# The first loop of a diffusion-transformer layer: adaLN columns, rstd and order of products rearranged

## The chip, the cores and the metric

The kernel runs on one core of one Trainium2 chip. The metric is the device time of one execution in microseconds (us); lower is better. A profiled execution also has a span, from its first to its last recorded instruction, which is a little shorter than its time. The engines are PE (matrix products; PEld is its weight load), DVE (VectorE), ACT (ScalarE), POOL (GpSimd) and SP (here only a queue that issues transfers).

## What is computed

One layer over 512 latent tokens and 256 context tokens of width 1024, in float32: a half-step SwiGLU feed-forward, a token mixing step (latent attention beside a gated MLP), and a second feed-forward. Each sublayer first normalises its input and then scales and shifts it (adaLN). Scale, shift and gate come from a conditioning vector c for the latent tokens and from a constant c_ctx for the context. The change touches only the beginning:

```python
mx = split((silu(c) @ w_ada + b_ada)[:, None, :], 9)          # latent: shift, scale, gate, ...
mc = split((silu(c_ctx) @ w_ada + b_ada)[None, None, :], 9)   # context
h = x * rsqrt(mean(x * x) + eps) * norm1_w
h = h * (1 + scale) + shift
x = x + 0.5 * gate * ((silu(h @ w1) * (h @ w3)) @ w2)         # width 1024 -> 2816 -> 1024
```

## The kernel before

Everything is kept transposed: the width of 1024 is cut into 8 tiles of 128 partitions (the index k or d below), and tokens lie along the free dimension, 512 latent and 256 context ones. A float32 product is made from three fast ones: each operand is split into a high part (a cast, on ScalarE) and a low part (a subtraction, on VectorE), and high x high, high x low and low x high are summed in PSUM. The names end in h and l: oph and opl for weights, hh and hl for the normalised input. The products of small float32 matrices that are not split run as two instructions each.

**Start (L253 to L307, L473 to L505).** SP's queue loads x's latent columns, then for tiles 0, 1 and 2 a block of w_ada (scale half and shift half, 1024 numbers a partition each) and a piece of the first feed-forward weights (wfirst), then the context columns of x. Meanwhile PE spreads c and c_ctx over all partitions (L478: 32 instructions with 128x128 weights), and ScalarE copies the result into cb (put_cb). ScalarE and VectorE square x, and PE adds over the width by a product with a matrix of ones (L486). So the sum of squares of each token stands in all 128 partitions, and rstd_start and rstd_end make rsqrt on arrays of 128x512.

**One adaLN tile d.** The scale of 128 output columns, for both conditioning vectors, is a row product (ada_row, L317): the weights are silu(c) and silu(c_ctx), 2 columns, and the moving operand is the block of w_ada, 128 wide; for d in ROWS2 = (1, 2, 3) the block holds the shift too and is 256 wide. The 2-row result is copied by ScalarE (ada_copy), turned into columns by PE with an identity (ada_col, L329), and gets bias and factor on ScalarE. For the other d the shift is a dot product on VectorE, one for each conditioning vector (ada_dot, 128x1024 with an accumulator, called junk in the profile).

**The first loop (L529 to L574).** It walks over k and makes the first two of the 22 feed-forward tiles: four latent products of 512 tokens with three parts each (first_mm, L524), which need hh and hl of tile k. For tile k + 1 VectorE multiplies x by scale and rstd (hfull), ScalarE adds the shift and casts (hh), VectorE makes hl. The context does the same one or two tiles at a time from k = 3 on (ctx_h), and its products (first_ctx, L517, 24 an iteration) come behind the latent products of the iteration after. The context's squares are made at k = 1 and 2 and added on VectorE; their sum over the width is taken on PE at k = 3 (L537).

**What sets the order.** The whole loop is written with the order of VectorE, ScalarE and GpSimd pinned (nc.ordered), and PE's instructions pinned one by one (pin). Each engine runs its own list in order, and a wait holds all that stands behind it on that engine. Buffers set when transfers start: two 1 MB blocks and one more in a side pool for w_ada, three raw buffers for weights; and there are five pairs of split weights (OPS), so the cast of tile 5 needs the pair that tile 0's context products read. SP issues its transfers in order too; an issue whose buffer is still in use holds the ones behind it.

After the loop come the rest of the first feed-forward, the mixing and the second feed-forward, where PE works almost without a gap. Their first product, in the profile, is the L60 row of PE at 76.06 us.

Of the kernel before, what the change touches and what calls it, by code (L numbers as in the profile page):

```python
# [17 lines left out]
P = 128  # L18
D = 1024
NK = D // P  # L20
# [6 lines left out]
EPS = 1e-6  # L27
# [5 lines left out]
NFIRST = 2  # L33
ROWS2 = (1, 2, 3)
W1 = 2 * NFIRST * P
NPLAIN1 = 4
NPLAIN2 = 4
BLOCKS = 2
# [4 lines left out]
COL_B, COL_N1, COL_N2, COL_N3 = 0, 72, 80, 88  # L43
# [130 lines left out]
def layer_kernel(ctx: ExitStack, tc: tile.TileContext, xT, wfirst, wst, wada, wuq, wkpe, cols, wrope, vnw, rope, out):  # L174
# [25 lines left out]
    def mm():  # L200
        return ps.tile([P, 512], F32, tag="mm", bufs=4, name=f"mm_{nc.next_id()}")
# [54 lines left out]
    for k in range(0, NK, 2):  # L256
        load_x(k, 2, slice(0, 256))

    def first_units(k):
        r, rw = st.block(wada, k, sp if k % 3 == 2 else None), st.raw()  # L260
        nc.sync.dma_start(rw[:, :W1], wfirst[k])
        return r, rw

    u0, rw0 = st.raw_pool.tile([P, 2048], F32, tag="block", bufs=BLOCKS, name="block_first"), st.raw()
    nc.sync.dma_start(u0[:, :D], wada[0][:, :D])
    nc.sync.dma_start(u0[:, D:], wada[0][:, D:])
    nc.sync.dma_start(rw0[:, :W1], wfirst[0])
    units = [(u0, rw0), first_units(1)]
    units.append(first_units(2))
# [43 lines left out]
    def ada_row(r, d, kts=range(NK)):  # L313
        n = 2 * P if d in ROWS2 else P
        o = pa[0:2, :n]
        for kt in kts:
            pin(nc.tensor.matmul(o, sc[:, kt, :], r[:, kt * n : kt * n + n], start=kt == 0, stop=kt == NK - 1))  # L317
        return o

    def ada_copy(o, d):  # L320
        n = o.shape[1]
        row = sp.tile([2, 2 * P], F32, tag="row", name=f"row_{d}")[:, :n]
        nc.scalar.copy(row, o)
        return row

    def ada_col(row, d):
        o = [pcol[:, 4 * d + 2 * i : 4 * d + 2 * i + 2] for i in range(2)]
        for i in range(2 if d in ROWS2 else 1):
            pin(nc.tensor.matmul(o[i], row[:, i * P : i * P + P], ident[0:2, 0:2], start=True, stop=True))  # L329
        nc.scalar.activation(  # L330
            pairs[0][1][:, d, :], o[0], AF.Identity, bias=b1n[:, d : d + 1], scale=col[:, COL_N1 + d : COL_N1 + d + 1])
        if d in ROWS2:
            nc.scalar.activation(pairs[0][0][:, d, :], o[1], AF.Identity, bias=col[:, d : d + 1])

    def ada_shift(r, d, alone=False):
        for which in range(2) if d not in ROWS2 else ():
            ada_dot(r[:, D:], d, which, accs[:, d, which : which + 1])
            if alone:
                nc.scalar.activation(mod_s[0][which][:, d : d + 1], accs[:, d, which : which + 1], AF.Identity, bias=col[:, d : d + 1])
            yield  # L340
        if not alone and d not in ROWS2:
            nc.scalar.activation(pairs[0][0][:, d, :], accs[:, d, :], AF.Identity, bias=col[:, d : d + 1])
# [95 lines left out]
    def square0(which, k, on_vector=False):  # L438
        sel, n, _ = parts[which]
        sq = sp.tile([P, n], F32, tag=f"sqx{which}", bufs=4 if which == 0 else NK, name=f"sq0_{which}{k}")  # L440
        if on_vector:
            nc.vector.tensor_mul(two(sq), sel(x, k), sel(x, k))
        else:
            nc.scalar.activation(two(sq), sel(x, k), AF.Square)
        return sq

    def rstd_start(which, pt):
        n = parts[which][1]
        t = lambda s: sp.tile([P, n], F32, bufs=1, name=f"{s}{which}")
        r0, v = t("r0"), t("v")  # L450
        nc.scalar.activation(r0, pt, AF.Abs_reciprocal_sqrt, bias=epsc, scale=1.0 / D)
        return pt, r0, v

    def rstd_end(pt, r0, v):
        nc.vector.scalar_tensor_tensor(v, pt, EPS * D, r0, ALU.add, ALU.mult)
# [4 lines left out]
    def first_x(k, which):  # L460
        sel = parts[which][0]
        nc.vector.scalar_tensor_tensor(sel(hf, k), sel(x, k), mod_a[0][which][:, k : k + 1], two(rs[which]), ALU.mult, ALU.mult)

    def first_h(k, which):
        sel = parts[which][0]
        nc.scalar.activation(sel(hh, k), sel(hf, k), AF.Identity, bias=mod_s[0][which][:, k : k + 1])

    def first_l(k, which):
        sel = parts[which][0]
# [4 lines left out]
    pa, pcol = mm(), mm()  # L474
    bb = [big() for _ in range(2)]
    for w in range(2):
        for kt in range(NK):
            pin(nc.tensor.matmul(bb[w][:, kt // 4, (kt % 4) * P : (kt % 4) * P + P], sc[:, kt, w : w + 1].to_broadcast([P, P]), ident,  # L478
                                 start=kt % 4 == 0, stop=True, skip_group_check=True))
    sumx = mm()  # L480
    put_cb = lambda w: nc.scalar.copy(cb[:, w, :], bb[w].rearrange("p g c -> p (g c)"))
    for k in range(0, NK, 2):
        sa = square0(0, k)
        sb = square0(0, k + 1, k in (2, 6))
        nc.vector.tensor_add(sa, sa, sb)
        pin(nc.tensor.matmul(sumx, ones, sa, start=k == 0, stop=k == NK - 2))  # L486
    put_cb(0)
    nc.vector.tensor_scalar_add(b1, col[:, COL_B : COL_B + 72], 1.0)
    nc.vector.tensor_mul(b1n, b1[:, NK : 2 * NK], col[:, COL_N1 : COL_N1 + NK])
    r0 = rstd_start(0, sumx)  # L490
    row = ada_copy(ada_row(units[0][0], 0), 0)
    shift = ada_shift(units[0][0], 0, True)
    next(shift)
    rs = [rstd_end(*r0)]
    ada_col(row, 0)
    ops = {}

    first_x(0, 0)
    ops[0] = st.operand(units[0][1][:, :W1])
    first_h(0, 0)  # L500
    first_l(0, 0)
    ada_row(units[1][0], 1, range(4))
    put_cb(1)
    for _ in shift:
        pass  # L505
# [14 lines left out]
    def first_mm(k, i):  # L520
        uh, ul = ops[k]
        c = slice(i * P, i * P + P)
        for m, (l, r) in enumerate(((uh, hh), (uh, hl), (ul, hh))):
            pin(nc.tensor.matmul(two(pbs[i]), l[:, c], lat(r, k), start=k == 0 and m == 0, stop=k == NK - 1 and m == 2))  # L524

    ctx_h = {3: (0, 1), 4: (2, 3), 5: (4, 5), 6: (6, 7)}
    sqx = {1: 4, 2: 8}
    sqs = []
    for k in range(NK):  # L529
        if k + 3 < NK:  # L530
            units.append(first_units(k + 3))
        later = k + 2 < NK
        for i in range(NFIRST):
            first_mm(k, i)
        if k == 3:
            sumx = mm()[:, :256]
            pin(nc.tensor.matmul(sumx, ones, sqs[0], start=True, stop=True))  # L537
        if k == 0:
            row = ada_copy(ada_row(units[1][0], 1, range(4, NK)), 1)
            first_mm(0, NFIRST)  # L540
        if k + 1 < NK:
            ada_col(row, k + 1)
        if later:
            o = ada_row(units[k + 2][0], k + 2)
        for i in range(NFIRST + (k == 0), 2 * NFIRST):
            first_mm(k, i)
        shift = ada_shift(units[k + 2][0], k + 2) if later else iter(())
        next(shift, None)
        if k + 1 < NK:
            first_x(k + 1, 0)  # L550
            ops[k + 1] = st.operand(units[k + 1][1][:, :W1])
            first_h(k + 1, 0)
            next(shift, None)
            first_l(k + 1, 0)
        if later:
            row = ada_copy(o, k + 2)
        next(shift, None)
        if k == 3:
            rs.append(rstd_end(*rstd_start(1, sumx)))
# [6 lines left out]
        for j in ctx_h.get(k - 1, ()):  # L566
            first_ctx(j)
        if k in sqx:
            while len(sqs) < sqx[k]:
                sqs.append(square0(1, len(sqs)))  # L570
                if len(sqs) > 1:
                    nc.vector.tensor_add(sqs[0], sqs[0], sqs[-1])
        if k == 5:
            nc.scalar.activation(epsc2, epsc, AF.Silu)  # L574
# [1273 lines left out]
```

## Time and profile before

| | us |
|---|---|
| median of 3 runs | 1159.21 |
| lowest and highest run | 1158.89, 1159.34 |
| profiled execution, its own time | 1157.46 |
| its span | 1155.7 |
| first product of the first loop | 17.55 |
| first product behind the loop | 76.06 |

How to read the rows: in the order of time, a row has the start, the duration, the engine, the line, the operation with the tile it writes and the tiles it reads, and in brackets the idle time of that engine before it and what ended it. Many operations are recorded by a helper, so their line is L60 and the tile names tell them apart. In the rows by stretches, the columns are the length, then busy time and number of instructions of PE, PEld, DVE, ACT and POOL, the clock that PE was granted, the busy share of the transfer engines, and GB/s. In rows of groups, the numbers behind the bar are the busy time, the mean duration of one in ns, then the idle time before them and what ended it. PE's products overlap, so their durations add up to more than the time they take; the distance between starts is the price.

### The profile page before, as it was taken

Reading aid. Unit: us, or ns where it says so; the run is one execution under the profiler, and the core shown is the slowest. Engines: PE = TensorE matmul, PEld = TensorE weight load, DVE = VectorE, ACT = ScalarE, POOL = GpSimd, SP = SyncE. Lnnn points to the kernel's source line nnn. Section 1 sums busy time; section 2 is a strip of 40 time slices with the busy share of each in tenths; the row PEclk is TensorE's granted clock in tenths of the full one; section 3 lists DMA queues with packets and bytes.
Section 4 is the critical chain, followed back from the end, with each engine's and each line's share of the span. In section 5 each row is a group of like instructions: output and inputs, shape, how many; then the busy total and the mean of one; then the engine's idle time right before and its main releaser. Section 6 shows DMA issues by size and latency. Waiting matters only on the chain. (4 is left out here: it accounts for less than half of the span.)

```text
span 1155.7 us, 18702 instructions
## 1 busy us (share of the span) xinstructions
PE 1137.7 (98%) x7070; PEld 1069.7 (93%) x7070; DVE 904.5 (78%) x1670; ACT 532.7 (46%) x1075; POOL 321.6 (28%) x277
## 2 busy tenths in 40 slices
PE   9999999999999999999999999999999999999998
PEld 5699999999999999999988788999999989898997
DVE  4778989888988878867746969869876959686884
ACT  4454431441344213444735549876553535353441
POOL 0001402320433013300017636670013425152330
PEclk9999999999999999999999999999999999999999
DMA  9440244344234665312242101002221322233312
GB/s 346 150 157 24 92 146 147 109 145 154 103 128 146 222 205 170 133 64 68 83 146 91 57 35 56 20 1 76 72 92 55 134 86 77 106 110 110 110 37 92
DMA packets 34650, 125.89 MB, mean 109 GB/s; under 512 B 3584, under 2 KB 10496, under 8 KB 29056
## 3 DMA queue, kind: packets, MB, share of 16 engines
q1 hardware_dynamic: 34416, 124.63, 31.4%
q8 instruction: 56, 0.92, 0.3%
q14 instruction: 34, 0.28, 0.1%
q10 hardware_dynamic: 144, 0.06, 0.0%
HBM read 122.58 MB, written 2.10 MB: 108 GB/s over the span
## 5 line engine op out<-in xcount | busy, mean ns | idle before, releaser
L60 POOL TENSOR_TENSOR block<-block 128x512 f32<-128x512 f32 x69 | 104.9, 1520 | 395.8 <-DVE opl L60 393.1
L60 DVE TENSOR_TENSOR opl<-block,oph 128x512 fp32r<-128x512 f32 x216 | 184.0, 858 | 32.1 <-ACT oph L60 30.0
L60 ACT CAST oph<-block 128x512 fp32r<-128x512 f32 x216 | 133.8, 621 | 144.4 <-PE mm L60 99.1
L60 PE MATMUL mm<-gh,oph 128*128 128x384 f32 (+1 forms) x440 | 155.2, 353 | 0.0
L60 PE MATMUL mm<-gl,oph 128*128 128x384 f32 (+1 forms) x440 | 154.9, 352 | 0.0
L60 PE MATMUL mm<-gh,opl 128*128 128x384 f32 (+1 forms) x440 | 154.9, 352 | 0.0
L60 DVE SCALAR_TENSOR_TENSOR x<-mm,g,x 128x256 f32<-128x256 f32 (+2 forms) x184 | 82.8, 489 | 48.5 <-PE mm L60 47.8
L60 ACT CAST oph<-raw 128x512 fp32r<-128x512 f32 x106 | 64.5, 619 | 93.4 <-PE mm L60 74.5
L60 POOL TENSOR_TENSOR block<-s,block 128x512 f32<-128x512 f32 x35 | 48.2, 1378 | 153.8 <-DVE opl L60 153.1
L60 PEld LDWEIGHTS mm<-gh,oph 128*128 128x128 f32 x440 | 82.6, 188 | 5.7
L60 PEld LDWEIGHTS mm<-gh,opl 128*128 128x128 f32 x440 | 82.6, 188 | 5.6
L60 PEld LDWEIGHTS mm<-gl,oph 128*128 128x128 f32 x440 | 82.6, 188 | 5.5
L60 DVE TENSOR_TENSOR opl<-raw,oph 128x512 fp32r<-128x512 f32 x106 | 71.0, 683 | 11.7 <-ACT oph L60 11.2
L60 PE MATMUL mm<-hl,oph 128*128 128x384 f32 x192 | 64.3, 335 | 0.9 <-DVE hl L60 0.9
L60 PE MATMUL mm<-hh,oph 128*128 128x384 f32 x192 | 64.5, 336 | 0.0
L60 PE MATMUL mm<-hh,opl 128*128 128x384 f32 x192 | 64.1, 334 | 0.0
L60 DVE SCALAR_TENSOR_TENSOR junk<-raw,cb 128x1024 bf16<-128x1024 f32 x48 | 63.2, 1331 | 0.0
L60 POOL TENSOR_TENSOR s<-block 128x512 f32<-128x512 f32 x34 | 51.1, 1504 | 19.8 <-DMA block<-wst 19.8
L60 PE MATMUL one<-hh,oph 128*128 128x384 f32 x144 | 48.1, 334 | 0.0
L60 PE MATMUL one<-hl,oph 128*128 128x384 f32 x144 | 48.1, 334 | 0.0
L60 PE MATMUL one<-hh,opl 128*128 128x384 f32 x144 | 48.1, 334 | 0.0
L60 DVE SCALAR_TENSOR_TENSOR raw<-raw,cb 128x1024 f32<-128x1024 f32 x32 | 41.0, 1287 | 7.6 <-DMA raw<-wada 7.4
(649 smaller groups left out, 3462.7 us busy)
## 6 DMA issues: line engine op xcount, KB each, us to landing
raw<-wst SPq DMA_DIRECT2D x77, 512.0 KB, 3.7
block<-wst SPq DMA_DIRECT2D x36, 1024.0 KB, 4.9
raw<-wada SPq DMA_DIRECT2D x56, 512.0 KB, 4.1
block<-wada SPq DMA_DIRECT2D x7, 1024.0 KB, 7.2
x<-xT SPq DMA_DIRECT2D x6, 512.0 KB, 7.0
raw<-wfirst SPq DMA_DIRECT2D x8, 256.0 KB, 6.2
out<-x SPq DMA_DIRECT2D x7, 256.0 KB, 2.5
block_first<-wada SPq DMA_DIRECT2D x2, 512.0 KB, 8.1
```

Source lines behind the costliest of these rows:

```text
L60: return lambda *a, **k: self.tc.keep_in_program_order(f(*a, **k))
```

## The change

It has five parts, all in the start and the first loop.

1. Scale columns: the roles of the operands are exchanged. The 128x128 block of w_ada is now the weights and silu(c), silu(c_ctx) the 2-wide moving operand (ada_pe, L320 of the new file, 8 products of two instructions each), so that the column comes out as it is needed; row, copy and transposes go.
2. Shift columns: VectorE dots for every tile but d = 1 (SHIFT_PE), where PE makes them in the same way as the scale. The dots for the context are placed by a table (ctx_shift). Scale halves, shift halves and wfirst pieces are loaded by separate transfers into buffers of their own: three for scales, two of two shifts each.
3. rstd on tokens in partitions: the squares are the weights and a column of ones the moving operand (L443), so the sum of a token stands in one partition; rstd is made on 128x4 (128x2 for the context), and PE spreads it over the rows (over_rows, L457) into PSUM, where VectorE reads it for the latent tokens. The last tile's squares are halved between VectorE and ScalarE, and the last pair of x's loads is cut in two.
4. The products of tile 0 are taken in halves of 256 tokens (first_half, L543), with the columns of tile 1 between the halves.
5. For k = 4 to 6 the context products stand ahead of the latent products of the same iteration, no longer behind them.

Nothing behind the loop is edited. The diff, cut to its core:

```diff
-ROWS2 = (1, 2, 3)
+SHIFT_PE = (1,)
...
     def first_units(k):
-        r, rw = st.block(wada, k, sp if k % 3 == 2 else None), st.raw()
+        ra = sp.tile([P, D], F32, tag="sa", bufs=3, name=f"scale_{k}")
+        nc.sync.dma_start(ra, wada[k][:, :D])
+        if k % 2 == 0:
+            sblk.append(st.raw_pool.tile([P, 2048], F32, tag="block", bufs=BLOCKS, name=f"shift_{k}"))
+        rs_ = sblk[-1][:, (k % 2) * D : (k % 2) * D + D]
+        nc.sync.dma_start(rs_, wada[k][:, D:])
+        rw = st.raw()
         nc.sync.dma_start(rw[:, :W1], wfirst[k])
...
-    def ada_row(r, d, kts=range(NK)):
-        n = 2 * P if d in ROWS2 else P
-        o = pa[0:2, :n]
-        for kt in kts:
-            pin(nc.tensor.matmul(o, sc[:, kt, :], r[:, kt * n : kt * n + n], start=kt == 0, stop=kt == NK - 1))
-        return o
+    def ada_pe(d, part, dst, **kw):
+        o = pcol[:, 4 * d + 2 * part : 4 * d + 2 * part + 2]
+        r = units[d][part]
+        for kt in range(NK):
+            pin(nc.tensor.matmul(o, r[:, kt * P : kt * P + P], sc[:, kt, :], start=kt == 0, stop=kt == NK - 1))
+        nc.scalar.activation(dst[:, d, :], o, AF.Identity, **kw)
...
+    def ada_shift(d, which):
+        if d in SHIFT_PE:
+            if which == 0:
+                ada_pe(d, 1, pairs[0][0], bias=col[:, d : d + 1])
+            return
+        ada_dot(units[d][1], d, which, accs[:, d, which : which + 1])
+        nc.scalar.activation(mod_s[0][which][:, d : d + 1], accs[:, d, which : which + 1], AF.Identity, bias=col[:, d : d + 1])
...
+    def sums(sq, c0, first, last):
+        for t in range(sq.shape[1] // P):
+            pin(nc.tensor.matmul(stats[:, c0 + t : c0 + t + 1], sq[:, t * P : t * P + P], ones[:, 0:1],
+                                 start=first and t == 0, stop=last, skip_group_check=True))
+    def over_rows(dst, r):
+        for t in range(r.shape[1]):
+            pin(nc.tensor.matmul(dst[:, t * P : t * P + P], r[:, t : t + 1].to_broadcast([P, P]), ident,
+                                 start=t == 0, stop=True, skip_group_check=True))
...
+    ctx_shift = {0: (0,), 1: (2,), 3: (3,), 4: (4,), 5: (5,), 6: (6, 7)}
     for k in range(NK):
+        n = k + 1
         if k + 3 < NK:
-            units.append(first_units(k + 3))
+            first_units(k + 3)
+        if k == 0:
+            first_half(0)
+        if n < NK:
+            ada_scale(n)
+            ada_shift(n, 0)
         if k == 3:
-            sumx = mm()[:, :256]
-            pin(nc.tensor.matmul(sumx, ones, sqs[0], start=True, stop=True))
+            sums(sqs[0], 4, True, True)
+            rc = rstd_tok(4, 2)
+        if k == 0:
+            first_half(1)
+        elif n < NK:
+            for j in ctx_h.get(k - 1, ()):
+                first_ctx(j)
+            first_mm(k)
+        else:
+            first_mm(k)
+            for j in ctx_h[k - 1]:
+                first_ctx(j)
+        if k == 3:
+            over_rows(stats[:, 256:512], rc)
+        if n < NK:
+            if k < 3:
+                oph(n)
+                opl(n)
+            first_x(n, 0)
+            first_h(n, 0)
+            if k >= 3:
+                oph(n)
+            for j in ctx_shift.get(k, ())[:1]:
+                ada_shift(j, 1)
+            first_l(n, 0)
+            if k >= 3:
+                opl(n)
+        for j in ctx_shift.get(k, ())[1:]:
+            ada_shift(j, 1)
+        if k in (1, 2):
+            while len(sqs) < (NK // 2 if k == 1 else NK):
+                sqs.append(square0(1, len(sqs)))
+        if k == 2:
+            for sq in sqs[1:]:
+                nc.vector.tensor_add(sqs[0], sqs[0], sq)
...
         for j in ctx_h.get(k, ()):
             first_x(j, 1)
             first_h(j, 1)
```

More of the change, by code (lines that the diff above doesn't have):

```diff
@@ L255, in layer_kernel @@
     load_x = lambda k, n, c: nc.sync.dma_start(four(x[:, k : k + n, :], c), four(xT[:, k : k + n, :], c))
-    for k in range(0, NK, 2):
-        load_x(k, 2, slice(0, 256))
+    for k, n in ((0, 2), (2, 2), (4, 2), (6, 1), (7, 1)):
+        load_x(k, n, slice(0, 256))
+    sblk, units = [], []
     def first_units(k):
-        r, rw = st.block(wada, k, sp if k % 3 == 2 else None), st.raw()
[L261 to L269, printed above, removed]
+        ra = sp.tile([P, D], F32, tag="sa", bufs=3, name=f"scale_{k}")
[5 more added lines that the diff above has]
+        rw = st.raw()
+        nc.sync.dma_start(rw[:, :W1], wfirst[k])
+        units.append((ra, rs_, rw[:, :W1]))
+    for k in range(3):
+        first_units(k)
     for k in range(0, NK, 4):
@@ L326, in ada_col @@
[L326 to L333, printed above, removed]
@@ L473, in layer_kernel, with c_rows, oph, opl @@
     nc.ordered = True
-    pa, pcol = mm(), mm()
+    stats, pcol, spread = mm(), mm(), mm()
     bb = [big() for _ in range(2)]
-    for w in range(2):
-        for kt in range(NK):
+    def c_rows(w, kts):
+        for kt in kts:
             pin(nc.tensor.matmul(bb[w][:, kt // 4, (kt % 4) * P : (kt % 4) * P + P], sc[:, kt, w : w + 1].to_broadcast([P, P]), ident,
                                  start=kt % 4 == 0, stop=True, skip_group_check=True))
-    sumx = mm()
     put_cb = lambda w: nc.scalar.copy(cb[:, w, :], bb[w].rearrange("p g c -> p (g c)"))
-    for k in range(0, NK, 2):
+    c_rows(0, range(NK))
+    c_rows(1, range(4))
+    for k in range(0, 6, 2):
         sa = square0(0, k)
-        sb = square0(0, k + 1, k in (2, 6))
+        sb = square0(0, k + 1)
         nc.vector.tensor_add(sa, sa, sb)
-        pin(nc.tensor.matmul(sumx, ones, sa, start=k == 0, stop=k == NK - 2))
-    put_cb(0)
+        if k == 2:
+            put_cb(0)
+            c_rows(1, range(4, NK))
+        sums(sa, 0, k == 0, False)
     nc.vector.tensor_scalar_add(b1, col[:, COL_B : COL_B + 72], 1.0)
     nc.vector.tensor_mul(b1n, b1[:, NK : 2 * NK], col[:, COL_N1 : COL_N1 + NK])
[L490 to L495, printed above, removed]
-    ops = {}
[L498 to L505, printed above, removed]
+    for k in (6, 7):
+        sums(square0(0, k), 0, False, k == 7)
+    r0 = rstd_tok(0, 4)
+    put_cb(1)
+    ops = {}
+    def oph(k):
+        ops[k] = st.pair()
+        nc.scalar.copy(ops[k][0], units[k][2])
+    def opl(k):
+        nc.vector.tensor_sub(ops[k][1], units[k][2], ops[k][0].bitcast(F32))
+    ada_scale(0)
+    over_rows(spread, r0)
+    rs = [spread]
+    oph(0)
+    ada_shift(0, 0)
+    for g in range(2):
+        first_x(0, 0, g)
+        first_h(0, 0, g)
+    first_l(0, 0, 0)
+    opl(0)
+    first_l(0, 0, 1)
     pbs = bigs(4)
```

109 lines of the change are left out of this document (42 added, 67 removed).

## The prediction

> **What bounds the kernel now.** I read the page first, then busy time by stretches around the first loop, then the groups and waits inside it, then its order of time.
>
> ```profile
> span 1155.7 us, 18702 instructions
> PE 1137.7 (98%) x7070; PEld 1069.7 (93%) x7070; DVE 904.5 (78%) x1670; ACT 532.7 (46%) x1075; POOL 321.6 (28%) x277
> ```
> ```profile
> 0.00:17.55 17.55, 15.65 (x73) 9.85 (x73) 9.21 (x19) 10.40 (x19) 0.69 (x6) 1.00 0.92 334
> 17.55:76.06 58.51, 56.21 (x319) 40.15 (x319) 40.45 (x73) 26.71 (x62) 0.00 (x0) 1.00 0.57 198
> 76.06:1155.70 1079.64, 1065.85 (x6682) 1019.71 (x6680) 854.87 (x1580) 495.61 (x996) 320.89 (x271) 1.00 0.29 100
> ```
> ```profile
> L317 PE MATMUL mm<-block,sc 128*2 128x256 f32 x48 | 11.0, 379 | 0.1
> L317 PE MATMUL mm<-block,sc 128*2 128x128 f32 x64 | 7.6, 272 | 0.0
> L329 PE MATMUL mm<-ident,row 2*128 2x2 f32 x22 | 3.7, 254 | 0.3 <-ACT row L60 0.3
> ```
>
> PE is busy everywhere, so only what shortens PE's sequence, or a wait in it, moves the end. The change lies in the first two stretches: start-up (to 17.55) and the first loop (to 76.06, where the next stage's first product begins). In the loop PE is busy 56.2 of 58.5 us, and the rows above are what the change can take: the adaLN columns. Order of time for the loop's last third:
>
> ```profile
> 53.21 0.62 ACT L60 CAST oph<-raw 128x512 fp32r<-128x512 f32 x1 [3.46 <-PE mm L517]
> ```
> ```profile
> 56.41 0.50 PE L524 MATMUL big<-hl,oph 128*128 128x512 f32 x1 [1.42 <-DVE hl L60]
> ...
> 58.08 1.91 PE L317 MATMUL mm<-block,sc 128*2 128x128 f32 x16
> 59.92 0.50 PE L524 MATMUL big<-hh,oph 128*128 128x512 f32 x1
> ...
> 61.41 0.28 PE L517 MATMUL mm<-hh,oph 128*128 128x256 f32 x1
> ...
> 64.29 0.40 PE L524 MATMUL big<-hh,oph 128*128 128x512 f32 x1
> ...
> 76.06 0.34 PE L60 MATMUL mm<-hh,oph 128*128 128x384 f32 x1
> ```
>
> From starts, not durations (PE is pipelined): 24 context products (L517) take 64.29 - 61.41 = 2.88 us, 0.12 each; a scale row of 16 instructions takes 59.92 - 58.08 = 1.84. The first row shows a wait the order makes: the cast for tile 5 needs a buffer that the context products free; PE then waits 1.42 us for what follows from it.
>
> ```profile
> 26.48 0.50 PE L524 MATMUL big<-hh,oph 128*128 128x512 f32 x1
> ...
> 26.82 0.39 PE L524 MATMUL big<-hl,oph 128*128 128x512 f32 x1
> 27.05 0.40 PE L524 MATMUL big<-hh,opl 128*128 128x512 f32 x1
> ```
> ```profile
> 22.41 0.52 PEld L329 LDWEIGHTS mm<-ident,row 2*128 2x128 f32 x4 [0.36 <-ACT row L60]
> 22.94 3.11 PEld L317 LDWEIGHTS mm<-block,sc 128*2 128x2 f32 x16
> 26.48 0.19 PEld L524 LDWEIGHTS big<-hh,oph 128*128 128x128 f32 x1 [0.44 <-issue]
> ```
>
> A latent product takes 0.23 us (26.82 to 27.05), so a tile's twelve take 2.75; the first after a float32 group takes 0.34, and with the gap ahead of it the change of kind costs 0.24. Back to float32 I take 0.1, between two float32 groups 0.06.
>
> **The change, part by part.**
>
> *Price of the new operation.* Columns now come from 128x128 float32 weights and a 2-wide moving operand: 16 loads per column and 16 tiny products. Before has no such group. The nearest row is the four L329 loads above, also 128 columns wide and followed by 2-wide products: (0.52 - 0.184)/3 = 0.112 us a load, 0.184 being one load's duration. The other end is the wide broadcast loads:
>
> ```profile
> 4.87 3.61 PEld L478 LDWEIGHTS big<-ident,sc 128*128 128x128 f32 x27
> ```
>
> (3.61 - 0.19)/26 = 0.1315, with 128-wide products between; that is also my price for the added broadcasts. I take 0.112, the row with 2-wide products, for columns and sums: 1.8 us a column. So a scale column costs what the 128-wide row did (1.84); what goes is the L329 transposes, the ScalarE row copies, and the doubled rows of d = 1, 2, 3 (3.6 us from 22.94 to 26.48), of which only d = 1 keeps its shift on PE (a second 1.8).
>
> *Start-up.* The 32 broadcast pairs end at 8.5 on PE (the L478 row). Sums over d now have x's squares as weights: five groups of 8 loads, 40 x 0.112 + 5 x 0.06 = 4.8, gives 13.3. PE is never without them: the last square starts at 9.89, on x's landing, and now halved between ScalarE and VectorE is there by about 11.
>
> ```profile
> 9.89 0.63 ACT L60 ACTIVATE sq<-x 128x512 f32<-128x512 f32 x1 [0.34 <-DMA x<-xT]
> ...
> 13.02 0.69 ACT L60 ACTIVATE r<-mm,epsc 128x512 f32<-128x512 f32 x1 [1.60 <-PE mm L486]
> ...
> 15.98 0.75 DVE L60 SCALAR_TENSOR_TENSOR hfull<-x,a,v 128x512 f32<-128x512 f32 x1
> ...
> 17.55 0.49 PE L524 MATMUL big<-hh,oph 128*128 128x512 f32 x1
> ```
>
> Before, rstd cost 2.96 us (13.02 to 15.98) on ScalarE and VectorE. Now it is four numbers a partition (under 1 us, beside PE's first scale column, 13.4 to 15.2), then eight broadcast loads spread it over rows (1.1, to 16.4). Half a tile follows: multiply 0.48, bias 0.50, hand-overs 0.2, first product about 17.7. Start-up gains nothing; its gain goes to sums, column and spread, all on PE in a row.
>
> *The queue on SP.* The stretch in which transfers are the bound is this:
>
> ```profile
> 10.00:30.00 20.00, 18.85 (x85) 9.12 (x85) 10.90 (x19) 8.39 (x19) 0.00 (x0) 1.00 1.05 385
> ```
> ```profile
> 31.17 0.33 SPq L261 DMA_DIRECT2D raw<-wfirst  x1
> ```
>
> Order and bytes up to the context's x are unchanged (7.1 MB, about 22 us); scale and shift are now issued apart, six issues more at 0.33 each, spread over the loop. Column 3 comes next, 0.5 MB later: about 26, and PE wants it at 30. Later columns wait for buffers that PE frees a round or more ahead (shift 6 and 7 for the last dot of tile 3, at 45, landing about 50; wanted at 54). I cost transfers at nothing; the cover is 3 to 4 us.
>
> *Iteration 0.* Twelve half products end about 19.3 (they wait a little for hl and opl), then two columns: 19.3 + 0.1 + 2 x 1.8 = 23.05. ScalarE's in-order queue has shift 1 ahead of the cast of tile 1, so that cast starts about 23.45, and VectorE's next step at 24.1.
>
> *VectorE's chain to the context sums.* Paces from starts:
>
> ```profile
> 58.13 1.22 DVE L60 SCALAR_TENSOR_TENSOR junk<-block,cb 128x1024 bf16<-128x1024 f32 x1
> ...
> 59.28 0.75 DVE L60 SCALAR_TENSOR_TENSOR hfull<-x,a,v 128x512 f32<-128x512 f32 x1
> 59.94 0.68 DVE L60 TENSOR_TENSOR opl<-raw,oph 128x512 fp32r<-128x512 f32 x1
> 60.55 1.22 DVE L60 SCALAR_TENSOR_TENSOR junk<-block,cb 128x1024 bf16<-128x1024 f32 x1
> ...
> 61.69 0.74 DVE L60 SCALAR_TENSOR_TENSOR hl<-hfull,s,hh 128x512 fp32r<-128x512 f32 x1
> ```
> ```profile
> 39.98 2.01 DVE L60 TENSOR_TENSOR sq<-sq,sq 128x256 f32<-128x256 f32 x4
> ```
> ```profile
> L60 ACT ACTIVATE hh<-hfull,s 128x512 fp32r<-128x512 f32 x8 | 5.8, 722 | 2.6 <-DVE hfull L60 2.6
> L60 ACT CAST oph<-raw 128x512 fp32r<-128x512 f32 x9 | 5.5, 612 | 3.5 <-PE mm L517 3.5
> ```
>
> Dot 1.14, multiply and hl 0.66 each, opl 0.61, a chained square sum 0.53. In program order to the sums: three opl, three multiplies, three hl (5.8), four dots (4.6), two waits in which shift and cast follow a dot on ScalarE (1.1 each), one for hh of tile 3 (0.93), and all seven square sums in one row (3.6): 17.1, so 24.1 + 17.1 = 41.2. Three of these dots (d = 2 and 3) are new: their shifts stood in PE's doubled rows. A wait of 1.1 is the dot's tail 0.16, a hand-over 0.1, the shift 0.2 and the cast. PE needs less: half products, column 2, tile 1, column 3, tile 2 and column 4 end at 37.0. It then **waits 4.2 us for the context sums**. Before, that wait was 1.03:
>
> ```profile
> 42.04 0.30 PEld L537 LDWEIGHTS mm<-sq,ones 128*128 128x128 f32 x2 [1.03 <-DVE sq L60]
> ```
>
> *From there.* Sums 0.5, tile 3 3.0 with its change of kind, spread 0.6, column 5 1.85: 47.2. Context products 0 and 1 now go ahead of tile 4; their hl comes 7.0 us after 41.2 (dot, rstd behind ScalarE, multiply, dot, hl, opl, context pair), 48.25 on PE. Then 2.88 + 2.75 to 53.9; twice column, context, tile (0.1 + 1.8 + 0.24 + 2.88 + 2.75 = 7.76) to 69.4; tile 7 and the last context, 5.63, to 75.05. The 1.42 us wait is gone, since the products that free the cast's buffer now stand ahead. The L524 row at 64.29 checks this way of adding: 2.75, two transposes with their changes of kind 0.55, 2.88, 2.75 and 2.88 give 76.1; the trace has 76.06. VectorE is never late after 48: its six to seven microseconds a round lie under PE's 7.76.
>
> *After the loop* every engine's order is the same, but one raw load that goes ahead of a block load on SP. VectorE's five opl for the next stage start behind the silu of tile 7, as now:
>
> ```profile
> 74.64 3.09 DVE L60 TENSOR_TENSOR opl<-raw,oph 128x512 fp32r<-128x512 f32 x5
> ```
>
> The first is done 0.7 us ahead of 76.06; in the new loop both shift alike, so the gain passes on.
>
> *Sum.* 76.06 - 75.05 = 1.0 us. The profiled execution took 1157.46 (span 1155.7); it would take 1156.5. The runs' median, 1159.21, lies 1.75 above it, so I carry the difference over: **1158.2**.
>
> **Rivals.**
>
> *Loads at the slower pace.* If 128-row weights load at 0.1315, each of the 124 on the path (40 sums, columns 0 and 1 and shift 1, four context sums, columns 6 and 7) costs 0.0195 more: +2.4, 1160.6. For it: that row has full 128x128 weights. Against: its products are 128 wide, not 2. Chance 0.12.
>
> *The wait is short.* If VectorE's chain is 3.2 us shorter (ScalarE's hops of 3.1 us covered, sums closer), the wait before the sums stays at the 1.0 of before and all behind it moves: 1155.0. For it: before, the same sums were nearly hidden. Against: the order, in which each dot's shift stands ahead of the next cast. From a chain 1.3 us shorter it is past 0.2%. Chance 0.22.
>
> *Loads don't overlap (the slower side).* If a load can't run under the product ahead of it, a pair costs at least the load's own 0.19: 0.076 more on 124, +9.4, 1167.6; past 0.2% from 0.140 a pair. Against: L329 above, four 0.184 loads in 0.52. For it only that no row has 128-row weights with 2-wide products. Chance 0.06. [...]
>
> *The wait cools PE.* The first broadcasts ran slow (0.2 us a load, against 0.1315 later):
>
> ```profile
> 3.84 1.36 PEld L478 LDWEIGHTS big<-ident,sc 128*128 128x128 f32 x6 [0.60 <-issue]
> ```
>
> If 4.2 us idle brings half speed back, 3.6 us of tile 3 do half their work: +1.8, of which the 1.05 us wait for context hl covers some: about 1159.0. Chance 0.08. [...]
>
> [...]
>
> *The gain is lost behind the loop* (the opl row's margin goes): 1159.2. Chance 0.06.
>
> **How the numbers follow.** Forecast 1158.2 with 0.46, its own range 1156.3 to 1159.6. A measurement here can tell about 0.2%, 2.3 us, so 1156.9 and 1161.5 are the bounds. Faster: the short wait (0.22) and the forecast's lower end (0.10): 0.32. Slower: no overlap (0.06), half-way between the paces and it (0.04): 0.10. Same: 0.58. The range reaches to 1154.6 (short wait) and 1160.8 (slower pace) and leaves out 0.18.
>
> **What would show it.** Right: L320 loads at 0.11; a PE wait of 3 to 5 us on VectorE's sq ahead of the context sums near 37; no wait for hl at tile 5; next stage's first product near 75. Wrong: L320 loads over 0.13, that wait under 2, or a first product of the loop away from 17.7.

## The result, and the profile after

The changed kernel is slower by 0.8%: 1168.11 us median of 6 runs (1164.82 to 1170.25), against 1159.05 (1157.73 to 1160.20) for the kernel before on the same chip. The ratio is 1.0076, with an interval of 1.0059 to 1.0094. The forecast of 1158.2 was 9.9 us too low. The profiled execution, the slowest of the six, took 1170.25, with a span of 1168.5.

The stretches of the changed kernel, cut at the same two products as before (columns: length; busy time and count of PE, PEld, DVE, ACT, POOL; granted clock; transfers):

```profile
0.00:17.55 17.55, 16.46 (x96) 15.27 (x97) 5.11 (x15) 9.35 (x16) 0.68 (x6) 0.84 0.93 331
17.55:87.17 69.62, 64.89 (x349) 59.61 (x348) 45.24 (x85) 27.24 (x66) 0.00 (x0) 0.75 0.51 167
87.17:1168.50 1081.33, 1067.12 (x6682) 1020.85 (x6680) 856.25 (x1581) 495.15 (x996) 317.47 (x271) 1.00 0.29 100
```

The loop ends at 87.17 instead of 76.06, which is 11.1 of the 12.8 us between the two spans. What strikes the eye is the granted clock: 0.84 and 0.75, where before had 1.00. The page's line of slices shows the same (before's was 9 from end to end):

```profile
PE   9999999999999999999999999999999999999998
...
PEclk7699999999999999999999999999999999999999
```

PE is 9 throughout: by its busy time nothing is wrong. The next fence makes that plain. First before, then after, 12 to 42 us:

```profile
12.00:42.00 30.00, 28.70 (x138) 15.70 (x138) 18.25 (x32) 13.11 (x33) 0.00 (x0) 1.00 0.87 307
```

```profile
12.00:42.00 30.00, 28.31 (x120) 26.77 (x120) 12.59 (x24) 8.56 (x21) 0.00 (x0) 0.50 0.74 251
```

PE is busy for 28.7 and 28.3 us of the 30, and in the changed kernel at exactly half the clock. Short stretches place the edges (a shorter form of the rows: length, PE, clock, transfers):

```profile
11.50:12.00 0.50, 0.50 (x6) 0.88 1.09 418
42.50:43.00 0.50, 0.50 (x6) 0.90 0.00 0
49.00:50.00 1.00, 0.00 (x0) 0.71 0.37 94
56.00:56.50 0.50, 0.50 (x3) 0.75 0.31 33
59.00:60.00 1.00, 0.86 (x5) 0.83 0.99 401
63.00:63.50 0.50, 0.50 (x5) 0.92 0.00 0
```

A mean of 0.88 over half a microsecond that begins at 1.00 and ends at 0.50 puts the fall at 11.88. In the same way the clock rises at 42.60, falls at 49.42, rises at 56.25, falls at 59.66 and rises at 63.08. The distances are 30.72, 6.82, 6.83, 3.41 and 3.42: 9, 2, 2, 1 and 1 times 3.41 us. So all six edges of this stretch lie on one grid of 3.41 us, and the clock between them is 1.00 or 0.50. A stretch between two neighbours on that grid is called a step from here on.

What PE did meanwhile (columns: start, duration, engine, line, operation, in brackets the idle time before):

```profile
9.19 4.66 PE L443 MATMUL mm<-ones,sq 128*128 128x1 f32 x32
13.71 3.55 PE L320 MATMUL mm<-sc,scale 128*128 128x2 f32 x16
17.12 2.05 PE L457 MATMUL mm<-ident,v 128*128 128x128 f32 x8
20.42 1.23 PE L543 MATMUL big<-hh,oph 128*128 128x256 f32 x4 [1.24 <-ACT hh L60]
...
36.98 0.63 PE L551 MATMUL big<-hl,oph 128*128 128x512 f32 x1
37.41 0.63 PE L551 MATMUL big<-hh,opl 128*128 128x512 f32 x1
...
46.70 1.84 PE L320 MATMUL mm<-sc,scale 128*128 128x2 f32 x16
51.45 1.01 PE L443 MATMUL mm<-ones,sq 128*128 128x1 f32 x4 [2.91 <-DVE sq L60]
...
66.76 1.84 PE L320 MATMUL mm<-sc,scale 128*128 128x2 f32 x16
68.46 0.36 PE L536 MATMUL mm<-hh,oph 128*128 128x256 f32 x1
```

The clock falls in the middle of the sums, whose moving operand is one column wide. By its duration, a column product costs 1.84 / 16 = 0.115 us a load at full clock (46.70) and 3.55 / 16 = 0.22 at half (13.71); from start to start it is 1.70 / 16 = 0.106 (66.76 to 68.46) and 3.41 / 16 = 0.21 (13.71 to 17.12). So the forecast's price of 0.112 was right, at the clock that it assumed.

Behind the loop the changed kernel took 1081.33 against before's 1079.64, although the orders there are the same:

```profile
667.00:670.65 3.65, 3.65 (x10) 0.53 0.01 4
```

One 3.41 us step at half clock, behind a stretch of 660 to 667 in which PE was busy for 4.92 us, costs 1.7. I don't count it to the change: the kernel before with the wide products (below), which has no part of it, reads 1.00 from 12 to 64 us and 0.999 over its span of 1168.2, about what one such step would take off (1.7 / 1168.2 = 0.0015).

### The profile page after: what moved, and what is told of

The parts are those of the page before. It is cut to its first block, busy times and chain, and to the rows that moved or that the text cites. A ratio compares the mean times of both kernels' runs of the same rounds, so it can differ in the third digit from the quotient of the medians.

```text
span 1168.5 us, 18838 instructions
## 1 busy us (share of the span) xinstructions
PE 1148.5 (98%) x7122; PEld 1095.7 (94%) x7122; DVE 906.6 (78%) x1679; ACT 531.7 (46%) x1076; POOL 318.2 (27%) x277
## 5 line engine op out<-in xcount | busy, mean ns | idle before, releaser
L60 POOL TENSOR_TENSOR block<-block 128x512 f32<-128x512 f32 x69 | 104.6, 1515 | 397.7 <-DVE opl L60 395.0
L60 DVE TENSOR_TENSOR opl<-block,oph 128x512 fp32r<-128x512 f32 x216 | 185.6, 864 | 33.2 <-ACT oph L60 31.0
L60 ACT CAST oph<-block 128x512 fp32r<-128x512 f32 x216 | 133.8, 621 | 143.9 <-PE mm L60 94.7
L60 PE MATMUL mm<-gh,oph 128*128 128x384 f32 (+1 forms) x440 | 155.2, 353 | 0.0
L60 PE MATMUL mm<-gl,oph 128*128 128x384 f32 (+1 forms) x440 | 154.9, 352 | 0.0
L60 PE MATMUL mm<-gh,opl 128*128 128x384 f32 (+1 forms) x440 | 154.9, 352 | 0.0
L60 DVE SCALAR_TENSOR_TENSOR x<-mm,g,x 128x256 f32<-128x256 f32 (+2 forms) x184 | 83.0, 489 | 49.2 <-PE mm L60 48.7
L60 ACT CAST oph<-raw 128x512 fp32r<-128x512 f32 x106 | 64.4, 619 | 89.9 <-PE mm L60 67.8
L60 POOL TENSOR_TENSOR block<-s,block 128x512 f32<-128x512 f32 x35 | 46.2, 1319 | 165.9 <-DVE opl L60 165.3
L60 DVE TENSOR_TENSOR opl<-raw,oph 128x512 fp32r<-128x512 f32 x106 | 71.0, 684 | 24.5 <-ACT oph L60 24.0
L60 PEld LDWEIGHTS mm<-gh,opl 128*128 128x128 f32 x440 | 82.6, 188 | 5.7
L60 PEld LDWEIGHTS mm<-gl,oph 128*128 128x128 f32 x440 | 82.6, 188 | 5.6
L60 PEld LDWEIGHTS mm<-gh,oph 128*128 128x128 f32 x440 | 82.6, 188 | 5.6
L60 PE MATMUL mm<-hl,oph 128*128 128x384 f32 x192 | 64.3, 335 | 0.6 <-DVE hl L60 0.6
L60 PE MATMUL mm<-hh,oph 128*128 128x384 f32 x192 | 64.5, 336 | 0.0
L60 PE MATMUL mm<-hh,opl 128*128 128x384 f32 x192 | 64.1, 334 | 0.0
L60 DVE SCALAR_TENSOR_TENSOR junk<-raw,cb 128x1024 bf16<-128x1024 f32 x48 | 62.2, 1309 | 0.0
L60 POOL TENSOR_TENSOR s<-block 128x512 f32<-128x512 f32 x34 | 50.9, 1496 | 20.1 <-DMA block<-wst 20.1
L60 PE MATMUL one<-hh,oph 128*128 128x384 f32 x144 | 48.1, 334 | 0.0
L60 PE MATMUL one<-hl,oph 128*128 128x384 f32 x144 | 48.1, 334 | 0.0
L60 PE MATMUL one<-hh,opl 128*128 128x384 f32 x144 | 48.1, 334 | 0.0
L60 DVE SCALAR_TENSOR_TENSOR raw<-raw,cb 128x1024 f32<-128x1024 f32 x32 | 41.0, 1289 | 5.1 <-DMA raw<-wada 4.7
```

The costliest lines, as they stand in the source:

```text
L60: return lambda *a, **k: self.tc.keep_in_program_order(f(*a, **k))
```

## The experiments

**The theory (S).** The clock is granted by the columns that PE streams in 3.41 us, not by its recorded busy time or by weight loads. A product with 1 or 2 moving columns streams nearly nothing, and a few of them side by side would halve the clock for what follows, as at 11.88. **Rivals.** L: the denser weight loads bring it down (PEld 15.27 busy in the start). W: PE's waits do (1.24 and 2.91 us). D: thin products are merely slow. M: the array's multiplications count, not the columns that stream.

M is out by before itself. Its row products (L317) do the same multiplications with the operands the other way round: for each of the 128 rows of the array 2 x 256 in 0.22 us, where the columns do 128 x 2 in 0.106. In the prediction's rows they fill PE from 22.94 to 26.48, more than 3.41 us, and before's clock is 1.00 all through the loop.

### Widen the thin products: 96, 64 and 32 columns

The same two columns of silu(c), and the same ones, are repeated; the extra result columns are not read. So the loads, their order and what PE waits for stay, and only the streamed columns change. W is 96, 64 or 32:

```diff
-        o = pcol[:, 4 * d + 2 * part : 4 * d + 2 * part + 2]
+        o = pcol[:, (d + part) % 4 * P : (d + part) % 4 * P + W].rearrange("p (n c) -> p n c", c=2)
...
-            pin(nc.tensor.matmul(o, r[:, kt * P : kt * P + P], sc[:, kt, :], start=kt == 0, stop=kt == NK - 1))
-        nc.scalar.activation(dst[:, d, :], o, AF.Identity, **kw)
+            v = sc[:, kt, :].unsqueeze(1).to_broadcast([P, W // 2, 2])
+            pin(nc.tensor.matmul(o, r[:, kt * P : kt * P + P], v, start=kt == 0, stop=kt == NK - 1))
+        nc.scalar.activation(dst[:, d, :], o[:, 0, :], AF.Identity, **kw)
...
-            pin(nc.tensor.matmul(stats[:, c0 + t : c0 + t + 1], sq[:, t * P : t * P + P], ones[:, 0:1],
+            pin(nc.tensor.matmul(stats[:, t * P : t * P + W], sq[:, t * P : t * P + P], ones[:, 0:W],
...
```

**Both at 96.** 

> The changed kernel with the moving operand of the column products (L320, 2 columns) and of the sums (L443, 1 column) repeated to 96 columns; the extra columns of the result are not read. Same number of products, weight loads and waits. Theory S (the granted clock falls because thin products stream few columns in a stretch of about 3.4 us): the granted clock stays 1.00 from 12 to 42 us, where the changed kernel showed 0.50; a drop is possible only around the wait for the context sums; first L60 product behind the loop at 75 to 78 instead of 87.17, time 1157 to 1161. Rival L (the weight loads, packed more densely in the start than before: PEld 15.3 busy of the first 17.6 us against 9.9, bring the clock down): loads are as dense as in the changed kernel, so clock 0.98 over the span and 1165 to 1171. Rival W (PE's waits bring it down: 1.24 us ahead of the first product and 2.91 us at the context sums): waits stay, so 1165 to 1171 as well.

Measured: 1156.56 (10 runs, 1155.54 to 1158.97) against 1159.00, ratio 0.998 (0.997 to 0.999); time and loop end are a little under what was expected. L and W are out as causes of the 30 us at half clock. PE's rows of this kernel (whose lines are one further), in the first fence, and VectorE's in the second:

```profile
16.94 0.74 PE L544 MATMUL big<-hh,oph 128*128 128x256 f32 x4 [1.24 <-ACT hh L60]
21.00 2.02 PE L321 MATMUL mm<-sc,shift 128*128 128x96 f32 x16 [0.44 <-ACT a L60]
...
40.60 0.69 PE L444 MATMUL mm<-ones,sq 128*128 128x96 f32 x4 [3.78 <-DVE sq L60]
```

```profile
37.09 3.46 DVE L60 TENSOR_TENSOR sq<-sq,sq 128x256 f32<-128x256 f32 x7
```

```profile
16.90:40.60 23.70, 18.62 (x128) 16.62 (x129) 15.13 (x28) 9.06 (x24) 0.00 (x0) 1.00 0.85 289
40.60:45.00 4.40, 4.40 (x14) 3.57 (x15) 3.82 (x9) 1.88 (x5) 0.00 (x0) 0.61 0.01 4
45.00:74.15 29.15, 29.01 (x199) 26.75 (x198) 25.34 (x47) 14.84 (x33) 0.00 (x0) 1.00 0.50 171
74.15:1153.80 1079.65, 1065.71 (x6682) 1019.78 (x6680) 854.78 (x1581) 495.09 (x996) 318.71 (x271) 1.00 0.29 100
```

This is the kernel that the prediction described. The clock holds to the wait for the context sums, and only there falls, for one step (0.61 over 4.4 us). The loop ends at 74.15. Against the changed kernel that is 13.0 us in the loop and 1.7 behind it, together the 14.7 between the spans. That sets the slowest execution of the one beside the fastest of the other; between the medians it is 11.55.

**Only the columns at 96.** 

> The changed kernel with only the column products (L320) at 96 moving columns; the sums (L443) stay at 1 column. Theory S: the 24 thin sums of the start still bring the clock down at about 12 us, but it comes back before 30 us since the columns now stream; first L60 product behind the loop at 78 to 83, time 1160 to 1166. Rivals L and W: as the changed kernel, 1165 to 1171 with the clock back at about 42 us.

Measured: 1162.85 (1158.64 to 1164.91), ratio 1.0031 (1.0017 to 1.0045); the loop of the profiled execution, the fastest of the ten, ended at 77.30. The thin sums bring the clock down, and the wide columns let it come back, in this execution after one step (short form of the rows, here and below):

```profile
13.80:17.24 3.44, 3.44 (x18) 0.50 1.05 410
17.24:41.10 23.86, 19.46 (x136) 1.00 0.82 267
```

**Only the sums at 96.** 

> The changed kernel with only the sums (L443) at 96 moving columns; the column products (L320) stay at 2 columns. Theory S: no drop at 12 us; the two columns of iteration 0, 3.7 us side by side, bring it at 20 to 30 us instead; first L60 product behind the loop at 79 to 85, time 1161 to 1168. If the columns alone were harmless: 1157 to 1161. Rivals L and W: drop at about 12 us as in the changed kernel, 1165 to 1171.

Measured: 1161.88 (1159.43 to 1163.26), ratio 1.0022 (1.0013 to 1.0032); loop end 81.95. Now column 0 and what follows it, with PE's wait of 1.25 us for hh in the same step, bring the clock down, 6.3 us later than the sums did and sooner than expected:

```profile
4.50:18.20 13.70, 11.87 (x100) 1.00 1.05 389
18.20:38.60 20.40, 19.96 (x83) 0.50 0.76 247
```

So each of the two thin kinds does it without the other; the same wait with wide columns (1.24 us in the fence of both at 96) did not. Neither run's time is a sum of parts, and the ten executions with wide columns only lie 6 us apart. Their mean clock tells why: 0.996 over the span in the profiled one, 0.991 in the six slowest, an estimated six steps at half clock in place of three. That the thin groups fall into the steps differently each time would explain it; no trace of those six shows it.

**Both at 64.** 

> As the first, with 64 moving columns instead of 96 for both. In the changed kernel the clock held through a stretch with 40% of its time streaming (73.3 to 76.7 us) and fell behind one with 38% (56.25 to 59.66). A product of two instructions with 64 columns streams about 48% of the 0.112 us from load to load. Theory S: holds, clock 1.00 from 12 to 42 us, time 1157 to 1161, and not slower than with 96 columns. If the limit is higher than half: clock down as in the changed kernel, 1163 to 1171. Rivals L and W: 1165 to 1171.

Measured: 1157.22 (1155.55 to 1158.40), ratio 0.9985 (0.9976 to 0.9994); loop end 75.92.

```profile
12.00:42.60 30.60, 24.27 (x179) 1.00 0.84 289
```

**Both at 32.** 

> As the runs with 96 and 64 moving columns, with 32 for the column products and the sums. A product of two instructions with 32 columns streams about a quarter of the time from load to load, below the 38% behind which the changed kernel's clock fell. Theory S (streamed columns decide the clock): the clock falls in the start as with 1 and 2 columns; first L60 product behind the loop at 80 to 88, time 1162 to 1171. If it was only the 1 and 2 wide forms that count as idle: clock 1.00 to the wait for the context sums, time 1156 to 1158 as with 64.

Measured: 1162.52 (1158.86 to 1165.60), ratio 1.0031 (1.0017 to 1.0045); loop end 81.81.

```profile
14.90:38.85 23.95, 22.26 (x92) 0.50 0.80 266
```

64 columns hold and 32 don't, although both runs have the same edit but for W. So here it went by the width streamed, not by the odd forms of 1 and 2 columns. An estimate of the share of time: at the very start six products of 256 columns of the same float32 kind take 2.93 us, so a column takes 1.9 ns; the first broadcasts behind them cost 0.2 to 0.22 us a load, where 0.12 is the price at full clock, so I take this for half clock. At full clock I take half of it, 0.95; before's row products of 256 columns, (26.48 - 22.94) / 16 = 0.22 us each at 1.00, give 0.86. 64 columns then stream an estimated 0.061 of the 0.12 us from load to load, a half, and 32 a quarter.

### The same thin products in the kernel before

```diff
+        if k == 2:
+            for _ in range(48):
+                pin(nc.tensor.matmul(warm[:, 0:W], ident, ones[:, 0:W], start=True, stop=True))
```

**W = 1.** 

> The kernel before, with 48 products added on PE at the head of iteration 2 of the first loop: 128x128 weights, ONE moving column, a result that nobody reads. It tells whether thin products do this in a kernel that has nothing else of the change. By themselves 96 instructions at 0.115 us are 11 us, of which up to 2 us of PE's later waits (1.03 and 1.42) are absorbed. Theory S: the granted clock falls to 0.50 within 3.4 to 6.8 us of the first of them, the rest of them run at the double price (about 0.21), and the clock comes back only behind some 3 to 7 us of wide products: 1174 to 1182, 4 to 10 us more than the same with 96 columns. Rival L (density of weight loads) and rival D (thin products are merely slow): the same time and the same clock as with 96 columns, within 1 us.

**W = 96.** 

> The same 48 added products with 96 moving columns instead of one: the same weights, the same number of loads. Theory S: granted clock 1.00 throughout, 1168 to 1171.5 (12 us for the products less up to 2 us of absorbed waits). Rival L: clock falls as with one column, and both runs are at 1174 to 1182.

Measured: thin 1177.47 (1176.44 to 1178.45), wide 1170.16 (1169.06 to 1170.82). Ratios to before: 1.0161 (1.0146 to 1.0176) and 1.0097 (1.0081 to 1.0114). The rows of PE and the stretches behind, thin first:

```profile
35.08 16.85 PE L535 MATMUL mm<-ones,ident 128*128 128x1 f32 x96
```

```profile
35.00:39.00 4.00, 4.00 (x38) 1.00 0.61 242
39.00:52.00 13.00, 13.00 (x63) 0.50 0.00 1
52.00:59.60 7.60, 7.60 (x27) 0.50 0.13 35
```

```profile
33.83 10.85 PE L535 MATMUL mm<-ones,ident 128*128 128x96 f32 x96
```

```profile
37.00:45.00 8.00, 8.00 (x71) 1.00 0.01 2
```

Products that stream 96 times as much are 7.3 us cheaper. With one column the clock is down 4 us after the first of them, and stays down for 7.6 us of ordinary work behind the last. L and D are out here too, without any other part of the change.

### The wait for the context sums

GpSimd adds the first four tiles' squares, and PE sums that and the last four one by one:

```diff
-        if k == 2:
+        if k == 1:
             for sq in sqs[1:]:
-                nc.vector.tensor_add(sqs[0], sqs[0], sq)
+                nc.gpsimd.tensor_add(sqs[0], sqs[0], sq)
...
-            sums(sqs[0], 4, True, True)
+            for sq in (sqs[0], *sqs[4:]):
+                sums(sq, 4, sq is sqs[0], sq is sqs[-1])
```

**With 96 columns.** 

> The changed kernel with 96 moving columns for column products and sums, and PE's wait for the context sums taken away: GpSimd, idle in the loop, adds the squares of the first four tiles, and PE sums that and each of the last four tiles by itself (20 products instead of 4; 7 adds of VectorE go, 3.46 us). With 96 columns alone PE waited 3.78 us there, and the clock fell for the next 3.4 us. Theory S with the wait as the second cause: no drop at all in the loop; PE spends about 2.3 us on sums in place of 3.78 + 0.69; VectorE's next chain starts about 2.5 us sooner; first L60 product behind the loop at 70.5 to 73 instead of 74.15, time 1152.5 to 1155.5. Rival: the wait is hidden by something else that is late there (the high part of tile 4): 1155.5 to 1157.

**The same, once more.** 

> The run with 96 columns and 20 context sums on PE once more (the same kernel), beside the next one: 1153 to 1156, clock 1.00.

Measured: 1154.24 (1152.96 to 1155.91), ratio 0.9962 (0.9949 to 0.9975), and again 1153.52 (1152.30 to 1154.85), ratio 0.9956 (0.9943 to 0.9969). It beats both kernels. PE's sums, and the stretches, in the first of the two:

```profile
39.34 2.51 PE L444 MATMUL mm<-ones,sq 128*128 128x96 f32 x20
```

```profile
0.00:10.40 10.40, 8.61 (x33) 1.00 0.84 280
10.40:19.60 9.20, 7.99 (x71) 1.00 1.05 391
19.60:73.34 53.74, 52.32 (x356) 1.00 0.62 202
```

No wait stands ahead of the sums any more, and the loop has no step at half clock. From the first product to the end it takes 53.7 us; with 96 columns alone it was 57.2, with its wait and its slow step. Of these 3.5 us only 0.8 show in the loop's end (73.34, a little later than expected), because this execution's first product came at 19.62 and not at 16.94. The reason is the start, and a trap of the view: ahead of the first record of the clock the column reads 1.00, but the prices say half (so the 0.84 further up is too high). PE's first rows of the second run, where it is the same:

```profile
1.03 2.93 PE L278 MATMUL mm<-ones 128*128 128x256 f32 x6 [1.03 <-DVE nhalf L224]
4.76 5.39 PE L486 MATMUL big<-ident,sc 128*128 128x128 f32 x24 [0.80 <-ACT sc L279]
```

5.39 / 24 is 0.22 a load, where 0.12 is the price at full clock.

**With the thin products as they are.** 

> The changed kernel with its thin products as they are (1 and 2 moving columns), and only the wait for the context sums taken away as in the run with 20 sums on PE. Theory S (streamed columns): the clock falls at about 12 us as in the changed kernel and comes back at 40 us or later; the 20 thin sums cost as much at half clock (20 products of two at about 0.21: 4.2 to 8 us) as the wait did; first L60 product behind the loop at 82 to 90, time 1163 to 1171. Rival W (PE's waits bring the clock down): clock 1.00 at least from 30 us on, first L60 product behind the loop at 74 to 79, time 1155 to 1160.

Measured: 1168.38 (1166.67 to 1169.51), ratio 1.0080 (1.0067 to 1.0094); loop end 83.27.

```profile
11.70:39.00 27.30, 25.61 (x113) 0.50 0.78 265
39.00:49.30 10.30, 10.30 (x73) 1.00 0.50 162
49.30:59.50 10.20, 10.06 (x51) 0.67 0.41 134
```

The wait is gone and the time stays. The twenty thin sums themselves ran at full clock, contrary to the expectation, and the clock fell again behind them. So W is out in the changed kernel itself.

**One more product ahead of the start.**

```diff
-    for i in range(3):
+    for i in range(4):
         nc.tensor.matmul(two(warm[:, :256]), ones, ones2, start=True, stop=True)
```

> The same with four instead of three products of 256 columns on ones at the very start (L278; two instructions each, 0.98 us a product at half clock). In the run with 20 context sums PE was idle for 0.76 us ahead of the first product with c (4.72, waiting for the small load of c), and the clock came up at 10.41 only; in the run with 96 columns alone there was no such gap and it came up at 3.96. Theory S: the gap makes the first stretches miss the mark, so the extra product brings the clock up one stretch of 3.4 us sooner in such executions: 1 to 2 us less in the median, 1152 to 1154. Rival: where c comes at 4.0 the extra product only delays (up to 0.9 us): 1154 to 1156.

Measured: 1153.92 (1152.63 to 1155.32), beside 1153.52 without: no difference. The profiled execution did end its loop sooner (first L60 product behind it at 70.67 instead of 73.14), but its span is only 1.3 shorter: behind the loop it took 1081.13 instead of 1079.96, without a step at half clock. Of the six executions the two slowest, 1155.02 and 1155.32, have a mean clock of 0.998, where all five without the product have 0.999 or 1.000. Why the gain is lost in these ways stays open.

## Why the prediction was wrong, point by point

1. **What bounds the loop.** Right, once the clock is held: PE and VectorE's chain, not transfers. With 96 columns PE's waits from 10 to 45 us are all on ScalarE or VectorE.
2. **The price, 0.112 a load.** Right at full clock (0.115, or 0.106 from start to start), wrong as a price for the whole loop. **This is the step that failed**: it took the price of a load from rows of before at full clock, and let it stand although the operation streams so much less that the clock fell to 0.50 (11.88). A column product by rows, as before had it (L317), streams 128 or 256 columns for each load; turned round it streams two. Where the sum had 0.112 the trace has 0.21 to 0.22, and the other products of those stretches pay nearly double as well: 0.43 us for 512 columns (36.98 to 37.41), where the sum had 0.23.
3. **Start: first product near 17.7.** With 96 columns 16.94 in one execution and 19.62 in another, mostly by when the clock first rises (last section), so the first is partly luck. In the changed kernel 20.42, which the prediction had named as a sign of being wrong.
4. **Iteration 0: shift 1 ends at 23.05.** With 96 columns it ends at 21.00 + 2.02 = 23.02, by two errors that cancel: the start was 0.8 us sooner, and from it to this end it took 6.08 us, not 5.35, with a wait of 0.44 that the sum did not have. In the changed kernel at 27.00 + 3.58.
5. **VectorE's chain to 41.2, and PE waits 4.2.** With 96 columns 37.09 + 3.46 = 40.55, and 3.78. In the changed kernel the wait was shorter, 2.91, because PE came to it 11.7 us later and VectorE's sum ended only 10.9 later.
6. **Loop end at 75.05, no wait for hl at tile 5.** 74.15 with 96 columns and 75.92 with 64, and no such wait in either. So the sum was within 1 us of a kernel whose clock falls for one step only. Some of this is luck too: the sum had no such step in it, and in the first of the two the start was 0.8 us sooner.
7. **The gain passes on.** Right with 96 columns: 1079.65 behind the loop, before 1079.64.
8. **The rivals.** "The wait cools PE" named the mechanism, a clock that falls, but tied it to PE's one long wait and priced it at 1.8 us. The wait does cool PE, for one step (0.61 in the fence above), and that version was still faster than before. The cause was the products that stood where PE looked busiest. "Loads don't overlap" had the time nearest to the result, 1167.6, and the wrong reason: loads do overlap, at 0.115. The chance of 0.10 for slower rested on that rival and the way half to it; a clock priced over all thin products was missing from the list.

What was in reach: the row of the first broadcasts at 0.2 us a load was quoted, as a sign of the half clock. So each new product could have been priced at 0.2 as well, and not PE's wait alone. The length of a step and the share below which the clock fell could not: before's clock reads 1.00 all through its loop and shows neither.

## What to carry to other kernels

When operands are exchanged so that the small one moves, price the product twice: by its loads at full clock, and at half (here 0.115 and 0.22 us a load). In the traces of this case the clock fell behind steps of 3.41 us in which columns streamed for an estimated 43% of the time or less. Where thin products leave less than that, repeat the moving operand and look at the clock again; here 64 or 96 columns cost as good as nothing (0.12 against 0.115 a load) and gave back 11 us. Look at the granted clock before the busy share: PE was busy for 28.3 of 30 us at half speed.

## What the runs showed of the hardware that was not expected

- The clock was lost to thin products while PE hardly idled (28.3 of 30 us busy at 0.50), and one low step was enough: the step from 56.25 to 59.66 of the changed kernel holds 16 two-column products beside 3 products of 512, 4 of 128 and 1 of 256 columns (a second starts 0.03 us before its end). An estimate with 0.229 us for a product of 512 columns (as at 44.38 and 44.61, two rows of L551), half of that for 256 and 0.12 for the float32 ones of 128 gives 0.69 + 0.48 + 0.11 = 1.3 of 3.41 us, 38%. The step from 73.32 to 76.73, with 3 of 512, 6 of 256 and the ends of two more, gives 1.6 us, 47%, and the clock held.
- In the changed kernel the clock came back with more of the time streaming than it had gone with: at half clock a product of 512 columns takes 0.43 us (36.98 to 37.41), at full clock 0.23 (44.38 to 44.61), so the same columns fill nearly twice the time. The step from 35.77 to 39.18 had 2.8 us of products of 512 columns and did not bring it back, and the next, with about 2.5 us, did. The same estimate can be made for every step of the thirteen traces, from the starts and widths of all PE products, with 0.427 us for 512 columns at half clock (36.98 to 41.25 are ten products), the same for 256 columns of a float32 instruction (the distance between single starts of L278), and half of both at full clock. At full clock the 18 steps behind which the clock fell streamed for 43% of their time or less, and those behind which it held for 40% or more. At half clock the steps that brought it back streamed for 73% or more, and those that did not for 77% or less. In columns, 73 to 77% at half clock are 37 to 38% at full clock. So in these traces one count of columns, an estimated 0.4 of what fits into a step at full clock, parts the steps both ways as nearly as this estimate can tell; it gives the two steps above 77% and 74%, the wrong way round by a little.
- The steps did not stand at the same place in each execution. The first rise, where the trace's clock record begins, came at 5.05 us in the changed kernel (two steps ahead of 11.88), 3.96 with 96 columns, and 10.41 in the first run with 20 context sums; in the second, of the same kernel, it lies near 9.95 by PE's rows (0.22 a load up to 9.98, and (10.85 - 9.98) / 8 = 0.11 behind it). Between 96 columns and the first of these, whose starts have the same instructions, it moved the first product by 2.7 us (16.94 to 19.62, of which 0.7 is a later start of the products with c, 4.72 for 4.00). That is 0.23% of the span and more than the 1.0 us that the change was forecast to gain.
